# Larger weight chunks, one raw tile for a seven-product unit, and four such units in every column block of gate and up

## The chip, the cores and the metric

The kernel runs on one core of a Trainium2 chip. The metric is device time in microseconds (us) of one execution; the median of three runs of the kernel before is 2080.19 us.

## The reference

One layer of a decoder for 256 tokens (two tiles of 128, called t = 0, 1) with a model width D of 2048:

```python
f1 = swiglu(rms_norm(h, ffn1_pre_norm), ffn1_w_gate, ffn1_w_up, ffn1_w_down)   # D_FF = 5504
h = h + 0.5 * rms_norm(f1, ffn1_post_norm)
m = hybrid_token_mixer(rms_norm(h, mix_pre_norm), ...)    # u @ w_in, two linear attentions, w_branch_*, w_out
h = h + rms_norm(m, mix_post_norm)
f2 = swiglu(rms_norm(h, ffn2_pre_norm), ffn2_w_gate, ffn2_w_up, ffn2_w_down)
h = h + 0.5 * rms_norm(f2, ffn2_post_norm)
# swiglu(x, g, u, d) = (silu(x @ g) * (x @ u)) @ d
```

Everything is in float32. Nearly all of the arithmetic is in the products with the weight matrices: gate and up (2048 x 5504 each), down (5504 x 2048), w_in (2048 x 11280), the two branch matrices (1024 x 2048) and w_out (2048 x 2048).

## The kernel before, in words

**One product.** A product of a 128x128 piece of activations with a 128x512 block of weights in float32 is made of three matmuls (`mm3`, lines 157 to 159): x-high times w-high, x-low times w-high, x-high times w-low. So each weight block is needed as a high part and a low part. It is read by a DMA on the queue of SP into a tile `raw`; ACT copies it, rounded, into `whi` (line 151); DVE subtracts `whi` from `raw` into `wlo` (line 153). A chunk is two blocks, 512 KB (`RW = 2 * CB`); there are five buffers each of `raw`, `whi` and `wlo` (`RING = 5`). A buffer of `raw` is free again when DVE has made the low part, one of `whi`/`wlo` when the last matmul that reads it is done. SP issues its DMAs in order, each when its `raw` buffer is free.

**A column block.** The gate and up matrices are worked through in 11 blocks of 512 columns (the last of 384) by `gemm_pair`: four PSUM tiles c[t][i] (i = 0 gate, 1 up) gather 16 rows of 128x512 weight blocks, in eight units U0 to U7 of two rows each. A plain unit is four blocks (two rows of gate, two of up), 8 products, 24 matmuls.

**A unit of seven products.** For some units the 2x2 block product (two token tiles, two matrices) is made with 7 products in place of 8, in the manner of Strassen (`Blocks.seven`): 21 matmuls on PE, at the price of weight sums on DVE. Its four raw blocks lie in two tiles `ra` and `rb`, read by four DMAs of 256 KB. DVE adds two pairs (`wsum` 0 and 1, 128x1024), then replaces a raw block by a sum (128x512), then makes `wsum` 2 (128x512). ACT makes the high parts of `ra` (line 278), of wsum 0 and 1 (line 280), of `rb` (line 282) and of wsum 2 (line 284); DVE makes the low parts of `ra`, `rb` (128x1024 each) and of the three sums (128x1536), all in line 243, where every DVE add of the class `Blocks` is recorded. The sums of the activations (`hkhi`, `hklo`) are made once for a matrix. `SUMS = (2, 4, 6)` makes three units of a column block sevens, `FOUR = (2, 4, 5, 6)` four. Before, the column blocks 1 to 10 of each half-step take FOUR and SUMS in turn (in ffn1 the even ones FOUR, in ffn2 the odd ones); the first block has none. The units stand in the order U0, U1 (gate half), S2, U1 (up half), S4, U3 (gate half), S5, U3 (up half), S6, U7 with four sevens; S is a seven.

**After a column block**, `close` (DVE) adds the shared products, ACT applies silu, DVE multiplies gate and up into `hn`, PE transposes it (line 397, 8 transposes, in the next block) and ACT copies it to `hT` (line 709).

**The other stages.** `down_proj` does the same for the down matrix, in two halves of 1024 columns. The mixer computes w_in in pairs of column blocks (`two`, through `gemm_pair`); beside five of these pairs, marked `late`, PE, DVE, ACT and POOL also do the attention, as coroutines that `side.pump` advances. `out_proj` does w_out. The residual stream `h` (eight 128x512 tiles) stays in SBUF; in the mixer its room is lent out and it is read back from the DRAM tiles `away`.

**The order on each engine** is set when the program is built: a scheduler with a model of its own takes the instructions of all engines and writes each engine's list. At run time each engine goes through its list in order.

Of the kernel before, what the change touches and what calls it, by code (L numbers as in the profile page):

```python
# [27 lines left out]
RW = 2 * CB  # L28
STEPS = ((3, 2, 2, 2), (6, 1, 1, 1))
RING = 5  # L30
AHEAD = 3
# [55 lines left out]
def kernel(ctx: ExitStack, tc: tile.TileContext, a: dict, out: bass.AP):  # L87
# [22 lines left out]
    h = [[hpool.tile([P, CB], F32, name=f"h{t}_{n}") for n in range(4)] for t in range(NT)]  # L110

    away = [[dram.tile([P, CB], F32, name=f"away{t}_{n}") for n in range(4)] for t in range(NT)]
# [10 lines left out]

    def ring_alloc(w):
        hi, lo = [ring.tile([P, RW], F32R, tag=s, name=nm(s))[:, :2 * w]
                  .rearrange("p (i c) -> p i c", i=2) for s in ("whi", "wlo")]
        return [(hi, lo)]

    def wload(src: bass.AP, w: int, apart=False):
        raw = ring.tile([P, RW], F32, tag="raw", name=nm("raw"))[:, :2 * w].rearrange(  # L130
            "p (i c) -> p i c", i=2)
        for i in range(2) if apart else [slice(0, 2)]:
            nc.sync.dma_start(raw[:, i, :], src[:, i, :])
        return raw, apart

    def wchunk(src: bass.AP, w: int, alloc=ring_alloc, raw=None):


        raw, apart = raw or wload(src, w)
        parts = alloc(w)  # L140
        if len(parts) == 1:
            hi, lo = parts[0]
            for i in range(2) if apart else [slice(0, 2)]:
                split_into(hi[:, i, :], lo[:, i, :], raw[:, i, :])
            return [(hi[:, i, :], lo[:, i, :]) for i in range(2)]
        for i, (hi, lo) in enumerate(parts):
            split_into(hi, lo, raw[:, i, :])
        return parts
# [12 lines left out]
    def gemm_block(w_dram, c0, w, lhs, nkt=KT, held=None, raws=(), ready=()):  # L161
# [4 lines left out]
        raws, ready = list(raws), list(ready)  # L166
        nb = -(-w // CB)
        step = 2 // nb
        pss = [[ps_tile(f"mm{t}") for _ in range(nb)] for t in range(NT)]

        def chunk(k0, alloc):
            if ready:
                return ready.pop(0)
            raw = raws.pop(0) if raws else None
            src = w_dram[k0 * P:(k0 + step) * P, c0:c0 + w]
            return wchunk(src.rearrange("(k p) c -> p k c", p=P) if nb == 1 else
                          src.rearrange("p (n c) -> p n c", n=nb), w // nb, alloc, raw)

        def mm(t, k0, parts):
            for i, part in enumerate(parts):  # L180
                kt = k0 + i % step
                mm3(pss[t][i // step][:, :w // nb], lhs(t, kt), part, kt == 0, kt == nkt - 1)

        if held is None:
            for k0 in range(0, nkt, step):
                parts = chunk(k0, ring_alloc)
                for t in range(NT):
                    mm(t, k0, parts)
                side.pump()
        else:  # L190
            kept = []
            for i, k0 in enumerate(range(0, nkt, 2)):
                kept.append((k0, chunk(k0, ring_alloc if i < RING else held)))
                mm(0, *kept[-1])
                side.pump()
            for k in kept:
                mm(1, *k)
                side.pump()
            side.flush()
# [45 lines left out]
    class Blocks:  # L245
# [19 lines left out]
        def seven(self, u, end):  # L265
            w, k0 = self.w, 2 * u
            ra, rb = [ring.tile([P, RW], F32, tag="raw", name=nm("raw"))[:, :2 * w]
                      .rearrange("p (i c) -> p i c", i=2) for _ in range(2)]
            wsum, hi, lo = [row_tile(n, d)[:, :, :w] for n, d in
                            (("wsum", F32), ("wsumh", F32R), ("wsuml", F32R))]  # L270

            nc.sync.dma_start(ra[:, 0, :], self.block(0, k0))
            nc.sync.dma_start(ra[:, 1, :], self.block(1, k0 + 1))
            nc.sync.dma_start(rb[:, 0, :], self.block(1, k0))
            nc.sync.dma_start(rb[:, 1, :], self.block(0, k0 + 1))
# [4 lines left out]
            nc.scalar.activation(hi[:, 0:2, :], wsum[:, 0:2, :], AF.Copy)  # L280
            add(rb[:, 0, :], wsum[:, 0, :], ra[:, 1, :])
            nc.scalar.activation(bhi, rb, AF.Copy)  # L282
            summed = add(wsum[:, 2, :], rb[:, 0, :], rb[:, 1, :])
            last[0] = nc.scalar.activation(hi[:, 2, :], wsum[:, 2, :], AF.Copy)  # L284
# [4 lines left out]
            first, second, third = [[(part[0][:, i, :], part[1][:, i, :]) for i in range(n)]  # L289
                                    for part, n in (((ahi, alo), 2), ((bhi, blo), 2), ((hi, lo), 3))]  # L290
# [5 lines left out]
            self.product((0, 0), self.lhs(0, k0 + 1), second[1])  # L296
            side.pump()
            self.product("p6", self.part("s2", u), second[0], end)
            self.product("p5", self.part("d", u), third[0], end)
            self.product("p7", self.part("s3", u), third[1], end)  # L300
            self.product((1, 0), self.lhs(1, k0 + 1), third[2])
# [21 lines left out]
    def first_of(w_dram, c0, w=CB):  # L323
        def chunk(i):
            return wchunk(w_dram[2 * i * P:2 * (i + 1) * P, c0:c0 + w]
                          .rearrange("(k p) c -> p k c", p=P), w)
        return chunk

    def gemm_pair(ws, w, lhs, sums, ready=(), following=(), raws=(), sevens=SUMS,
# [11 lines left out]
        def split(i, k0):  # L341
            return wchunk(None, w, raw=raws.pop(0)) if raws else first_of(*ws[i], w)(k0 // 2)

# [11 lines left out]
        ready = list(ready)  # L355
        for j, (u, i) in enumerate(steps):
# [7 lines left out]
            parts = ready.pop(0) if ready else split(i, k0)  # L364
            if (u, i) == (nu - 1, 0) and sevens:
                ready = [split(1, k0)]
                b.share()
            for t in range(NT):
                b.plain((k0, k0 + 1), t, i, parts, u == nu - 1)
            side.pump()  # L370
        ready = [chunk(0) for chunk in following]
# [162 lines left out]
    def out_proj(w_dram, nkt, lhs, post, scale, pre, homes, following):  # L534
# [8 lines left out]
        def load(kt, hf, alloc=ring_alloc):  # L543
            return wchunk(w_dram[kt * P:(kt + 1) * P, hf * 1024:(hf + 1) * 1024]
                          .rearrange("p (n c) -> p n c", n=2), CB, alloc)

        def mm(t, n, kt, parts):
            if acc[t][n] is None:
                acc[t][n] = ps_tile(f"acc{t}{n}")
            mm3(acc[t][n], lhs(t, kt), parts[n % 2], kt == 0, kt == nkt - 1)  # L550

        order = [(kt, hf) for hf in range(2) for kt in range(2)]
        order += [(kt, hf) for kt in range(2, nkt - TAIL) for hf in range(2)]
        for i, (kt, hf) in enumerate(order):
            parts = load(kt, hf)
            if 6 <= i < 10:
# [5 lines left out]
                load_bcast(wpost[-1], post, i - 6, last[0])  # L562
            for t in range(NT):
                for n in (2 * hf, 2 * hf + 1):
                    mm(t, n, kt, parts)
            if i == 1:
                side.flush()
        tail = [[(kt, load(kt, hf, homes[hf * TAIL + i]))
                 for i, kt in enumerate(range(nkt - TAIL, nkt))] for hf in range(2)]

        for t in range(NT):
            ss = small.tile([P, 4], F32, tag="ss", name=nm("ss"))
            for n in range(4):
                for i, (kt, parts) in enumerate(tail[n // 2]):
# [12 lines left out]
    def down_proj(w_dram, nkt, lhs, sums_of, post, pre, wpost, ys, homes, following):  # L587
# [8 lines left out]
        def split(hf, kt, alloc=ring_alloc):  # L596
            return wchunk(w_dram[kt * P:(kt + 1) * P, hf * 1024:(hf + 1) * 1024]
                          .rearrange("p (n c) -> p n c", n=2), CB, alloc)
# [18 lines left out]
        ahead = []  # L617
        for hf in range(2):
# [6 lines left out]
            kt = 0  # L625
            while kt < n:
                u = kt // 2
                if kt % 2 == 0 and u + 1 in units and u + 1 not in parts:
                    parts[u + 1] = sums_of(u + 1)
                if u in units:  # L630
                    b.seven(u, u == units[-1])
                    kt += 2
                    continue
                chunk = ahead.pop(0) if ahead else split(hf, kt)
                if kt == 2 * units[-1] + 2:
                    ahead = [split(hf, kt + 1)]
                    b.share()
                if not hf and kt in (8, 9, 10, 11):
                    load_bcast(wpost[kt - 8], post, kt - 8, last[0])
                for t in range(NT):  # L640
                    for i in range(2):
                        b.plain((kt,), t, i, chunk[i:i + 1], kt == nkt - 1)
                if not hf and kt == 1:
                    side.flush()
                kt += 1
# [717 lines left out]
```

## Time and profile before

| | |
|---|---|
| runs | 2079.95, 2080.19, 2080.34 us |
| profiled execution | 2080.67 us, span 2078.8 us, granted clock of PE 0.999 |
| PE, matmuls | 2067.8 us busy, 99% |
| DVE | 1854.7 us busy, 89% |
| ACT | 1239.7 us busy, 60% |
| DMA | 412 MB, mean 198 GB/s |

The span is what the profile shows of the execution; the rest of its 2080.67 us, 1.9 us, lies around it. "Busy" of PE counts matmuls that overlap in the pipeline once. Rows of a timeline give the start, the duration, the engine, the line, and what was written from what; a duration of a pipelined instruction is longer than the step to the next start.

### The profile page before, as it was taken

To read this page: it belongs to the slowest core of one execution; us is meant where nothing else is said; L and a number is where in the kernel's file an instruction comes from. 1 tells how busy PE (TensorE), PEld (TensorE's weight loads), DVE (VectorE), ACT (ScalarE), POOL (GpSimd) and SP (SyncE) were. 2 spreads that over 40 slices of the span, in tenths; PEclk is the share of its full clock that TensorE was granted. 3 is DMA by queue.
4 is the path that set the end of the run, shared out by engine and by line. 5 is a ranking of instruction groups with operands and counts; after the bars stand their busy time and mean duration, and the time that the engine had idled before them with its cause. 6 is when DMAs were issued, how large, how long until landed. Compare 5 with 4: busy or idle time off the path is not lost.

```text
span 2078.8 us, 29319 instructions
## 1 busy us (share of the span) xinstructions
PE 2067.8 (99%) x10509; PEld 1721.1 (83%) x10509; DVE 1854.7 (89%) x2187; ACT 1239.7 (60%) x1670; POOL 40.6 (2%) x87
## 2 busy tenths in 40 slices
PE   9999999999999999999999999999999999999998
PEld 7888888898888888878888888888888888898886
DVE  7898999989999879989999897578999989999896
ACT  6555656565666576576655554465555655666663
POOL 1000000000000100000000000010000000000000
PEclk9999999999999999999999999999999999999999
DMA  8566656656667467555565666755666657576663
GB/s 267 183 210 199 211 188 194 214 183 226 208 195 233 153 192 232 163 168 188 174 203 186 184 221 214 220 179 172 222 200 186 209 186 224 165 239 201 198 208 132
DMA packets 200665, 412.23 MB, mean 198 GB/s; under 512 B 18036, under 2 KB 26423, under 8 KB 200520
## 3 DMA queue, kind: packets, MB, share of 16 engines
q1 hardware_dynamic: 194896, 401.80, 61.0%
q10 hardware_dynamic: 5624, 8.57, 1.3%
q8 instruction: 82, 1.34, 0.3%
q14 instruction: 63, 0.52, 0.1%
HBM read 406.11 MB, written 4.19 MB: 197 GB/s over the span
## 4 chain that ended last, share of the span: by engine, by line
PE 96%; ACT 1%; DVE 1%; issue 0%; DMA 0%; POOL 0%; SPq 0%; DVEq 0%; POOLq 0%; ACTq 0%
PE c L157 22%; PE c L159 21%; PE c L158 21%; PE p L159 5%; PE p L158 5%; PE p L157 5%; PE mm L157 3%; PE mm L159 3%; PE mm L158 3%; PE ps L397 2%; PE acc L157 1%; PE acc L158 1%; PE acc L159 1%; PE ps L905 0%; DVE h L510 0%
## 5 line engine op out<-in xcount | busy, mean ns | idle before, releaser
L151 ACT ACTIVATE whi<-raw 128x1024 fp32r<-128x1024 f32 (+3 forms) x498 | 510.6, 1033 | 279.8 <-PE c L158 114.7
L153 DVE TENSOR_TENSOR wlo<-raw,whi 128x1024 fp32r<-128x1024 f32 (+3 forms) x498 | 587.5, 1190 | 86.6 <-ACT whi L151 85.3
L157 PE MATMUL c<-whi,xhi 128*128 128x512 f32 (+1 forms) x1270 | 495.8, 391 | 0.5 <-DVE hq L849 0.3
L159 PE MATMUL c<-wlo,xhi 128*128 128x512 f32 (+1 forms) x1270 | 490.8, 387 | 0.0
L158 PE MATMUL c<-whi,xlo 128*128 128x512 f32 (+1 forms) x1270 | 490.5, 386 | 0.0
L243 DVE TENSOR_TENSOR wlo<-raw,whi 128x1024 fp32r<-128x1024 f32 (+1 forms) x252 | 294.5, 1203 | 11.9 <-ACT whi L278 6.3
L159 PEld LDWEIGHTS c<-wlo,xhi 128*128 128x128 f32 x1270 | 238.4, 188 | 47.2 <-DVE wlo L153 0.3
L157 PEld LDWEIGHTS c<-whi,xhi 128*128 128x128 f32 x1270 | 238.5, 188 | 46.9 <-issue 0.7
L158 PEld LDWEIGHTS c<-whi,xlo 128*128 128x128 f32 x1270 | 238.6, 188 | 44.9
L282 ACT ACTIVATE whi<-raw 128x1024 fp32r<-128x1024 f32 (+1 forms) x126 | 131.8, 1046 | 204.5 <-DVE raw L243 78.5
L243 DVE TENSOR_TENSOR wsuml<-wsum,wsumh 128x1536 fp32r<-128x1536 f32 (+1 forms) x126 | 218.0, 1730 | 33.7 <-ACT wsumh L284 33.6
L157 PE MATMUL c<-whi,hkhi 128*128 128x512 f32 x558 | 217.0, 389 | 0.0
L159 PE MATMUL c<-wlo,hkhi 128*128 128x512 f32 x558 | 216.8, 388 | 0.0
L158 PE MATMUL c<-whi,hklo 128*128 128x512 f32 x558 | 216.7, 388 | 0.0
L280 ACT ACTIVATE wsumh<-wsum 128x1024 fp32r<-128x1024 f32 (+1 forms) x126 | 131.5, 1044 | 108.6 <-DVE wsum L243 74.7
L278 ACT ACTIVATE whi<-raw 128x1024 fp32r<-128x1024 f32 (+1 forms) x126 | 131.4, 1043 | 100.2 <-PE c L158 84.7
L243 DVE TENSOR_TENSOR wsum<-raw,raw 128x1024 f32<-128x1024 f32 (+1 forms) x126 | 151.8, 1205 | 20.5 <-DMA raw<-in_ffn_w_down_dram 17.3
L159 PEld LDWEIGHTS c<-wlo,hkhi 128*128 128x128 f32 x558 | 104.8, 188 | 21.6
L158 PEld LDWEIGHTS c<-whi,hklo 128*128 128x128 f32 x558 | 104.8, 188 | 21.3
L157 PEld LDWEIGHTS c<-whi,hkhi 128*128 128x128 f32 x558 | 104.8, 188 | 21.3
L243 DVE TENSOR_TENSOR c<-c,psum 128x512 f32<-128x512 f32 (+1 forms) x135 | 86.6, 682 | 11.8 <-PE c L159 11.4
L243 DVE TENSOR_TENSOR wsum<-raw 128x512 f32<-128x512 f32 (+1 forms) x126 | 86.0, 683 | 3.6
(347 smaller groups left out, 3117.1 us busy)
## 6 DMA issues: line engine op xcount, KB each, us to landing
raw<-in_ffn_w_down_dram SPq DMA_DIRECT2D x124, 512.0 KB, 4.6
raw<-in_w_in_dram SPq DMA_DIRECT2D x104, 512.0 KB, 4.5
raw<-in_ffn_w_up_dram SPq DMA_DIRECT2D x97, 512.0 KB, 4.5
raw<-in_ffn_w_gate_dram SPq DMA_DIRECT2D x96, 512.0 KB, 4.7
raw<-in_ffn_w_gate_dram SPq DMA_DIRECT2D x128, 256.0 KB, 3.8
raw<-in_w_in_dram SPq DMA_DIRECT2D x128, 256.0 KB, 3.5
raw<-in_ffn_w_up_dram SPq DMA_DIRECT2D x126, 256.0 KB, 3.8
raw<-in_ffn_w_down_dram SPq DMA_DIRECT2D x96, 256.0 KB, 4.0
```

The lines of the kernel that those rows point to most:

```text
L151: last[0] = nc.scalar.activation(hi, src, AF.Copy)
L153: nc.vector.tensor_tensor(lo, src, hi.bitcast(F32), op=ALU.subtract)
L157: nc.tensor.matmul(ps, lhsT=xhi, rhs=whi, start=start, stop=False)
L158: nc.tensor.matmul(ps, lhsT=xlo, rhs=whi, start=False, stop=False)
L159: nc.tensor.matmul(ps, lhsT=xhi, rhs=wlo, start=False, stop=stop)
L243: return nc.vector.tensor_tensor(o, x, y, op=op)
L278: nc.scalar.activation(ahi, ra, AF.Copy)
L280: nc.scalar.activation(hi[:, 0:2, :], wsum[:, 0:2, :], AF.Copy)
L282: nc.scalar.activation(bhi, rb, AF.Copy)
L397: end = nc.tensor.transpose(dst_ps[:, i * P:(i + 1) * P], src[:, i * P:(i + 1) * P], ident)
```

## The change

Chunks grow from two blocks to four (`RW = 4 * CB`, 1 MB), and the buffers become fewer: three of `whi`/`wlo` (12 blocks where there were 10) and two of `raw` (8 blocks where there were 10). A plain unit is loaded into one raw tile by two DMAs of 512 KB, gate and up, and split by one ACT instruction and one DVE instruction of 128x2048. A seven has all four raw blocks in one tile: ACT copies three of them at once (line 291), then the fourth, which has become a sum (line 294), then the three weight sums at once (line 296); DVE makes the low parts of the four blocks at once. `h` is written to DRAM (`away2`, or taken from the input x again) after the first column block of each half-step, and its room serves as two more raw tiles, so there are four (16 blocks) from there until `residual()` in the second half of `down_proj`; in the mixer, in `out_proj` and in the first column block there are two. To make room, `hn` shares the tiles of `silu` and some other pools shrink. All ten column blocks of gate and up after the first take FOUR.

```diff
-RW = 2 * CB
+RW = 4 * CB
-RING = 5
-AHEAD = 3
+RING = 3
+RAWS = 2
+AHEAD = 2
...
+    def raw_tile(w):
+        turn[0] += 1
+        if roomy[0] and turn[0] % (RAWS + NT) >= RAWS:
+            raw = hpool.tile([P, RW], F32, tag="hold", name=nm("raw"), bufs=NT)
+        else:
+            raw = ring.tile([P, RW], F32, tag="raw", name=nm("raw"), bufs=RAWS)
+        return raw[:, :4 * w].rearrange("p (i c) -> p i c", i=4)
...
         def seven(self, u, end):
-            (ahi, alo), (bhi, blo) = ring_alloc(w) + ring_alloc(w)
-            nc.scalar.activation(ahi, ra, AF.Copy)
-            add(wsum[:, 0:2, :], ra, rb[:, 0:1, :].broadcast_to([P, 2, w]))
-            nc.scalar.activation(hi[:, 0:2, :], wsum[:, 0:2, :], AF.Copy)
-            add(rb[:, 0, :], wsum[:, 0, :], ra[:, 1, :])
-            nc.scalar.activation(bhi, rb, AF.Copy)
-            summed = add(wsum[:, 2, :], rb[:, 0, :], rb[:, 1, :])
-            last[0] = nc.scalar.activation(hi[:, 2, :], wsum[:, 2, :], AF.Copy)
+            raw = raw_tile(w)
+            for j, (i, k) in enumerate(((0, k0), (1, k0 + 1), (0, k0 + 1), (1, k0))):
+                load(raw, j, self.block(i, k))
+            hi, lo = ring_alloc(w)[0]
+            nc.scalar.activation(hi[:, 0:3, :], raw[:, 0:3, :], AF.Copy)
+            add(wsum[:, 0:2, :], raw[:, 0:2, :], raw[:, 3:4, :].broadcast_to([P, 2, w]))
+            add(raw[:, 3, :], wsum[:, 0, :], raw[:, 1, :])
+            nc.scalar.activation(hi[:, 3, :], raw[:, 3, :], AF.Copy)
+            summed = add(wsum[:, 2, :], raw[:, 3, :], raw[:, 2, :])
+            last[0] = nc.scalar.activation(shi, wsum, AF.Copy)
             with tc.issue_after(summed.ins):
-                add(alo, ra, ahi.bitcast(F32), ALU.subtract)
-            add(blo, rb, bhi.bitcast(F32), ALU.subtract)
-            add(lo, wsum, hi.bitcast(F32), ALU.subtract)
+                add(lo, raw, hi.bitcast(F32), ALU.subtract)
+            add(slo, wsum, shi.bitcast(F32), ALU.subtract)
...
-                        (FOUR if f0 // CB % 2 == fours else SUMS) if f0 else ())
+                        FOUR if f0 else ())
                 else:
                     g = gemm_block(a[pre + "_w_gate"], f0, w, xl, held=held, ready=ready)
+                    for t in range(NT):
+                        nc.sync.dma_start(away2[t], hrow[t])
...
+                roomy[0] = True
...
+            def residual():
+                roomy[0] = False
+                new_h()
+                for t in range(NT):
+                    nc.sync.dma_start(hrow[t], a["x"][t * P:(t + 1) * P, :].rearrange(
+                        "p (n c) -> p n c", c=CB) if begin else away2[t])
```

The order on ACT in column block 6 of ffn1 (four sevens before and after), from the high part of S2's first blocks to S4's last. Before, `raw_498`/`raw_499` are S2's two raw tiles and `raw_514`/`raw_515` those of S4; `hT` is the copy of the transposed block 5:

```order
L278 ACTIVATE whi_503_2447<-raw_498_2438 128x1024
L728 ACTIVATE silu_484_2371<-c00_415_2029,r_65_414 128x512
L728 ACTIVATE silu_485_2373<-c10_417_2031,r_67_421 128x512
L280 ACTIVATE wsumh_501_2441<-wsum_500_2440 128x1024
L282 ACTIVATE whi_505_2449<-raw_499_2439 128x1024
L284 ACTIVATE wsumh_501_2441<-wsum_500_2440 128x512
L151 ACTIVATE whi_512_2488<-raw_511_2486 128x1024
L278 ACTIVATE whi_519_2513<-raw_514_2504 128x1024
L709 ACTIVATE hT_486_2375<-ps_493_2408 128x4x128
L709 ACTIVATE hT_486_2375<-ps_494_2414 128x4x128
L282 ACTIVATE whi_521_2515<-raw_515_2505 128x1024
```

After, `raw_350` is S2's raw tile, `raw_360` that of S4, `raw_366` that of U3:

```order
L291 ACTIVATE whi_354_2208<-raw_350_2200 128x1536
L771 ACTIVATE silu_339_2136<-c10_292_1826,r_57_396 128x512
L291 ACTIVATE whi_364_2263<-raw_360_2255 128x1536
L746 ACTIVATE hT_340_2138<-ps_345_2169 128x4x128
L746 ACTIVATE hT_340_2138<-ps_346_2175 128x4x128
L294 ACTIVATE whi_354_2208<-raw_350_2200 128x512
L296 ACTIVATE wsumh_352_2202<-wsum_351_2201 128x1536
L164 ACTIVATE whi_367_2297<-raw_366_2294 128x2048
L294 ACTIVATE whi_364_2263<-raw_360_2255 128x512
```

S2's remaining high parts stood ahead of everything of S4; now S4's first copy and the two of hT stand ahead of them.

PE at the same S2, its first four products. Before:

```order
L157 MATMUL p1_507_2461<-whi_503_2447,xhi0_1_107 128x512
L158 MATMUL p1_507_2461<-whi_503_2447,xlo0_2_108 128x512
L159 MATMUL p1_507_2461<-wlo_504_2448,xhi0_1_107 128x512
L157 MATMUL c01_490_2381<-whi_503_2447,hkhi_85_524 128x512
L158 MATMUL c01_490_2381<-whi_503_2447,hklo_86_525 128x512
L159 MATMUL c01_490_2381<-wlo_504_2448,hkhi_85_524 128x512
L157 MATMUL c00_489_2380<-whi_505_2449,xhi0_1_107 128x512
L158 MATMUL c00_489_2380<-whi_505_2449,xlo0_2_108 128x512
L159 MATMUL c00_489_2380<-wlo_506_2450,xhi0_1_107 128x512
```

and after:

```order
L170 MATMUL p1_356_2218<-whi_354_2208,xhi0_3_97 128x512
L171 MATMUL p1_356_2218<-whi_354_2208,xlo0_4_98 128x512
L170 MATMUL c01_342_2142<-whi_354_2208,hkhi_66_483 128x512
L171 MATMUL c01_342_2142<-whi_354_2208,hklo_67_484 128x512
L170 MATMUL c00_341_2141<-whi_354_2208,xhi0_3_97 128x512
L171 MATMUL c00_341_2141<-whi_354_2208,xlo0_4_98 128x512
L170 MATMUL p6_357_2219<-whi_354_2208,hkhi_66_483 128x512
L172 MATMUL p1_356_2218<-wlo_355_2209,xhi0_3_97 128x512
L172 MATMUL c01_342_2142<-wlo_355_2209,hkhi_66_483 128x512
L172 MATMUL c00_341_2141<-wlo_355_2209,xhi0_3_97 128x512
```

Seven matmuls with high parts now stand ahead of the first one that needs S2's low part; before there were two.

DVE in a late pair of the mixer, the one beside the first attention output (`on`). Before, `raw_1745` and `raw_1746` are its first seven's raw tiles, `raw_1761` and `raw_1762` the second's:

```order
L243 TENSOR_TENSOR wlo_1753_8420<-raw_1746_8409,whi_1752_8419 128x1024
L987 SCALAR_TENSOR_TENSOR on_1741_8387<-ps_1736_8374,r_1740_8385,h1_0_85 128x256 x2
L243 TENSOR_TENSOR wsuml_1749_8412<-wsum_1747_8410,wsumh_1748_8411 128x1536
L153 TENSOR_TENSOR wlo_1760_8459<-raw_1758_8456,whi_1759_8458 128x1024
L243 TENSOR_TENSOR wsum_1763_8476<-raw_1761_8474,raw_1762_8475 128x1024
L243 TENSOR_TENSOR raw_1762_8475<-wsum_1763_8476,raw_1761_8474 128x512
```

After, `raw_1238` is the first seven's tile and `raw_1251` the second's:

```order
L259 TENSOR_TENSOR wlo_1243_7547<-raw_1238_7538,whi_1242_7546 128x2048
L1041 SCALAR_TENSOR_TENSOR on_1231_7507<-ps_1224_7491,r_1230_7505,h0_810_4883 128x256 x2
L259 TENSOR_TENSOR wsuml_1241_7541<-wsum_1239_7539,wsumh_1240_7540 128x1536
L1041 SCALAR_TENSOR_TENSOR on_1237_7523<-ps_1232_7510,r_1236_7521,h1_811_4884 128x256 x2
L166 TENSOR_TENSOR wlo_1250_7585<-raw_1248_7581,whi_1249_7584 128x2048
L259 TENSOR_TENSOR wsum_1252_7601<-raw_1251_7600 128x1024
```

The instructions stand in nearly the same order, but with two raw tiles `raw_1251` is the room of `raw_1238`: its DMAs can go out only after the first row, and the last row waits for them.

More of the change, by code (lines that the diff above doesn't have):

```diff
@@ L266, in seven @@
             w, k0 = self.w, 2 * u
[L267 to L274, printed above, removed]
@@ L295, in seven @@
             self.product((0, 1), self.part("s4", u), first[1])
-            self.product((0, 0), self.lhs(0, k0 + 1), second[1])
+            self.product((0, 0), self.lhs(0, k0 + 1), first[2])
             side.pump()
[L298 to L301, printed above, removed]
+            self.product("p6", self.part("s2", u), first[3], end)
+            self.product("p5", self.part("d", u), second[0], end)
+            self.product("p7", self.part("s3", u), second[1], end)
+            self.product((1, 0), self.lhs(1, k0 + 1), second[2])
             side.pump()
@@ L363, in gemm_pair @@
             k0 = 2 * u
[L364 to L367, printed above, removed]
+            if i == 0:
+                cuts = ()
+                if raws:
+                    raw, cuts = raws.pop(0)
+                    hi, lo = ring_alloc(w)[0]
+                    parts = [(hi[:, j, :], lo[:, j, :]) for j in range(4)]
+                else:
+                    parts = ready or split(load_unit(ws, u, w), w)
+                    ready = None
+                if u == nu - 1 and sevens:
+                    b.share()
+            for c in cuts[i] if cuts else ():
+                split_into(hi[:, c, :], lo[:, c, :], raw[:, c, :])
             for t in range(NT):
-                b.plain((k0, k0 + 1), t, i, parts, u == nu - 1)
+                b.plain((k0, k0 + 1), t, i, parts[2 * i:2 * i + 2], u == nu - 1)
             side.pump()
-        ready = [chunk(0) for chunk in following]
+        ready = following and following()
         for i in range(2 if sevens else 0):
@@ L549, in mm, with all_of @@
                 acc[t][n] = ps_tile(f"acc{t}{n}")
[L550 to L556, printed above, removed]
+            mm3(acc[t][n], lhs(t, kt), parts[n], kt == 0, kt == nkt - 1)
+        def all_of(ns, *chunks):
+            for kt, parts in chunks:
+                for t in range(NT):
+                    for n in ns:
+                        mm(t, n, kt, parts)
+        begun = []
+        for kt in range(2):
+            begun.append((kt, chunk(kt)))
+            all_of((0, 1), begun[-1])
+        side.flush()
+        all_of((2, 3), *begun)
+        for kt in range(2, nkt - TAIL):
+            parts = chunk(kt)
+            if 3 <= kt < 7:
                 if not free:
@@ L561, in out_proj @@
                 wpost.append(free.pop(0))
[L562 to L569, printed above, removed]
+                load_bcast(wpost[-1], post, kt - 3, last[0])
+            all_of(range(4), (kt, parts))
+        tail = [(kt, chunk(kt, homes[i])) for i, kt in enumerate(range(nkt - TAIL, nkt))]
         for t in range(NT):
@@ L624, in down_proj @@
             units = sorted(DSUMS + DMORE[hf])
[L625 to L628, printed above, removed]
+            for kt in range(0, n, 2):
+                u, m = kt // 2, min(2, n - kt)
+                if u + 1 in units and u + 1 not in parts:
                     parts[u + 1] = sums_of(u + 1)
```

261 lines of the change are left out of this document (144 added, 117 removed).

## The prediction

> **What bounds the kernel now.** I read the page's busy times first, then the chain that ended last, then what PE waits for.
>
> ```profile
> span 2078.8 us, 29319 instructions
> PE 2067.8 (99%) x10509; PEld 1721.1 (83%) x10509; DVE 1854.7 (89%) x2187; ACT 1239.7 (60%) x1670; POOL 40.6 (2%) x87
> PEclk9999999999999999999999999999999999999999
> PE 96%; ACT 1%; DVE 1%; issue 0%; DMA 0%; POOL 0%; SPq 0%; DVEq 0%; POOLq 0%; ACTq 0%
> ```
>
> PE holds 96% of the chain at full granted clock. The longest single waits of PE in the whole run are small:
>
> ```profile
> PE ps L1303 <- POOL idle L1298: 1.3, 1, 1.3
> PE ps L965 <- ACT state L975: 0.4, 1, 0.4
> PE c L157 <- DVE hq L849: 0.3, 1, 0.3
> ```
>
> So the time can fall only through fewer matmuls, and rises with every new wait of PE: 2067.8 of 2078.8 us is PE, and of the other 11 us the change touches little (the settling and the output at the end keep their instructions).
>
> DVE is the second limit. Two neighbouring column blocks of ffn1, three sevens (first) and four (second); the columns are PE, PEld, DVE, ACT, POOL, clock, DMA share, GB/s:
>
> ```profile
> 145.37:187.75 42.38, 42.38 (x193) 35.18 (x192) 38.63 (x39) 25.60 (x31) 0.00 (x0) 1.00 0.60 188
> 187.75:229.47 41.72, 41.72 (x189) 34.62 (x189) 39.99 (x41) 23.09 (x28) 0.00 (x0) 1.00 0.65 213
> ```
>
> The windows end where the transposes of `hn` end; the block lengths are thus 42.38 and 41.72 us. PE is busy throughout both. DVE works 38.63 us in the one and 39.99 in the other, where it has 1.73 us left.
>
> **The gain: matmuls removed.** Ten more sevens replace ten plain units, each with one product, three matmuls, less: 27 of 128x512 and 3 of 128x384 (ffn2's last block). What a matmul costs on a saturated PE is the step from start to start, not its duration of 0.39:
>
> ```profile
> 192.39 0.39 PE L157 MATMUL p<-whi,hkhi 128*128 128x512 f32 x1
> ...
> 194.89 0.39 PE L159 MATMUL c<-wsuml,xhi 128*128 128x512 f32 x1
> ```
>
> Eleven steps in 2.50 us, 0.227 each. The difference of the two blocks above, 0.66 us, is three matmuls by 0.22: four sevens gave their whole gain there. 27 x 0.227 + 3 x 0.17 (three quarters) = 6.6 us. Nothing else lies on PE's path to be removed, so 2080.2 - 6.6 = 2073.6 is the floor.
>
> **DVE and ACT in a block of four sevens.** The rows by form for the second window:
>
> ```profile
> L153 DVE TENSOR_TENSOR wlo<-raw,whi 128x1024 fp32r<-128x1024 f32 x9 | 10.9, 1216 | 0.0
> L243 DVE TENSOR_TENSOR wsuml<-wsum,wsumh 128x1536 fp32r<-128x1536 f32 x4 | 7.0, 1755 | 1.4 <-ACT wsumh L284 1.4
> L243 DVE TENSOR_TENSOR raw<-wsum,raw 128x512 f32<-128x512 f32 x4 | 2.8, 692 | 0.1
> L282 ACT ACTIVATE whi<-raw 128x1024 fp32r<-128x1024 f32 x4 | 4.2, 1057 | 11.0 <-DVE raw L243 3.9 <-issue 3.9 <-PE c L159 3.1
> L284 ACT ACTIVATE wsumh<-wsum 128x512 fp32r<-128x512 f32 x3 | 1.8, 615 | 0.0
> ```
>
> On DVE 692, 1216 and 1755 ns for 512, 1024 and 1536 columns: 0.53 per 512 more, so 128x2048 is estimated at 2.29 us. Instructions that follow each other overlap: a group of two of 1024 lasts 2.35 and the next starts 2.27 after its start, 1.13 each.
>
> ```profile
> 192.38 2.35 DVE L243 TENSOR_TENSOR wlo<-raw,whi 128x1024 fp32r<-128x1024 f32 x2
> 194.65 1.22 DVE L153 TENSOR_TENSOR wlo<-raw,whi 128x1024 fp32r<-128x1024 f32 x1
> ```
>
> Merging two of 1024 into one of 2048 so saves about 0.07 us, eight times a block: 0.55 us, and DVE comes to 39.4 of 41.7. Off PE's path this is worth nothing by itself; it pays for the waits below. [...]
>
> What changes more is where DVE waits. Before, 1.4 us a block for the copy of the third sum. Now ACT's lists in the order above put S4's first copy ahead of S2's last one, and S4's copy needs a `whi` buffer; with three, that is U0's. Count from the end of U0 on PE (zero). ACT starts about 0.10 after the last reader of the high part ends, as here:
>
> ```profile
> 194.66 0.39 PE L158 MATMUL c<-wsumh,xlo 128*128 128x512 f32 x1
> ...
> 195.15 1.06 ACT L280 ACTIVATE wsumh<-wsum 128x1024 fp32r<-128x1024 f32 x1 [0.28 <-PE c L158]
> ```
>
> That reader starts two steps before the end, so ACT starts at 0.04. The copy of 1536 columns takes about 1.39 (1.06 for 1024 and 0.43 for 512 more, less the overlap with the next), the two `hT` copies 0.95, S2's last copy of 512 columns 0.62, and DVE's 128x2048 2.29 more: S2's low part is there at 5.3 to 5.4. PE has meanwhile 8 transposes and 12 matmuls of U1, then the seven high matmuls of S2 that the new order puts ahead:
>
> ```profile
> 186.88 0.87 PE ps L397 x8
> ```
>
> 0.87 + 19 x 0.227 = 5.2. PE waits about 0.16 us. (In the old order, with two ahead, it would be 0.87 + 14 x 0.227 = 4.05 and a wait of 1.3.) The same count gives the low parts of S4, S5 and S6 0.4 to 0.6 us to spare. Eighteen blocks follow another block of four: 18 x 0.16 = 2.9 us. Both sides are sums of some five terms, so I bound it by 0 and 0.4 a block, 0 to 8 us.
>
> **Two raw tiles in the mixer, `out_proj` and the first blocks.** Loads wait for DVE to free a raw tile, now as before, but a mixer pair has 8 blocks of room for 10 and frees 4 at a time. The reload of one tile, by the times to landing:
>
> ```profile
> raw<-in_w_in_dram SPq DMA_DIRECT2D x104, 512.0 KB, 4.5
> raw<-in_w_in_dram SPq DMA_DIRECT2D x128, 256.0 KB, 3.5
> ```
>
> Two of 512 KB, or four of 256 KB that SP issues about 0.38 apart, land in some 4.6 to 5.4 us. Then a plain unit needs ACT's copy (1.9) and DVE's 2.29: 8.8 to 9.6. A seven needs two adds, the copy of the fourth block and the low part, 1.25 + 0.73 + 0.62 + 2.29: 9.5 to 10.3. Two tiles serve two units of PE, 48 or 45 or 42 matmuls, 10.9 or 10.2 or 9.5 us. It just fits where ACT and DVE are free at once; where DVE is full it does not. It is full in the attention stage:
>
> ```profile
> 835.00:1000.00 165.00, 164.59 (x1345) 133.07 (x1333) 156.53 (x234) 110.14 (x190) 7.09 (x12) 1.00 0.55 170
> ```
>
> 95% of 165 us. In the late pair shown in the order above, the second seven's load starts when the first's low part is made; until it lands, 4.6 to 5.4 us later, DVE has the two `on` (1.6), the sums' low part (1.67) and one plain low part (2.2), 5.5 us when all stand ready, 3.9 when the attention's are done: a hole of 0 to 1.3 us. Before it ran without one from there on:
>
> ```profile
> 906.04 1.22 DVE L153 TENSOR_TENSOR wlo<-raw,whi 128x1024 fp32r<-128x1024 f32 x1
> 907.17 1.22 DVE L243 TENSOR_TENSOR wsum<-raw,raw 128x1024 f32<-128x1024 f32 x1
> ```
>
> Ten pairs by 0 to 0.8 us, since only what outlasts PE's lead counts: 0 to 8, and I take 1 because attention matmuls stretch PE's side of these pairs. `out_proj` has 24 matmuls to each chunk (5.4 us, two tiles 10.9 against 9.6), the start of the kernel was waiting for DMA anyway, the last part of `down_proj` likewise has plain chunks: together 0 (0 to 2). The copies of `h` to DRAM and back, 2 MB each, go out beside a DMA share of 0.65: nothing, unless SP's queue holds the loads behind them.
>
> **Sum.** -6.6 + 2.9 + 1 + 0 = -2.7. Against the profiled 2080.67 that is 2078.0; the median is 0.5 lower, so 2077.5 us.
>
> **The rivals.**
> - A, all hidden: the reordered matmuls cover S2's low part and the raw tiles reload in time. For it: PE waits for nothing today. 2073.6 to 2075.
> - B, the mixer starves for raw tiles: what speaks for it is the reload plus the split at 9.5 to 10.3 against 9.5 to 10.9, and a DVE at 95%; against it, that PE in the late pairs does attention too. Ten pairs by 1 us and 2 for the other stages: +12 - 6.6 + 1 = 2086.6.
> - C, DVE becomes the bound of gate and up (the other side): it has 39.4 us of work in 41.7, and all blocks are alike now, without one of three sevens (DVE 38.63 of 42.38) between in which to catch up. From 2.3 us of waiting in a block on, DVE sets its length. S2's last copy, at 3.0 us from zero, is a wait of DVE, and three more sevens each have one. At 3.3 us: 1 us by 20 blocks, less 6.6: 2093.6. Against it: before it waited 1.4.
> - D, the new sevens just do not pay: DVE's waits come to some 0.35 us on PE in each of the 20 blocks: 2080.
>
> [...]
>
> **How the numbers follow.** Chances: forecast (2075 to 2080) 0.42, A 0.22, B 0.20, C 0.11, D 0.05. A measurement of this kernel tells 0.2%, 4.2 us, from nothing: faster is below 2076.0, slower above 2084.4. Faster: A and 0.18 of the forecast, 0.40. Slower: 0.17 of B and 0.09 of C, 0.26. Within: 0.34. The range runs from the floor less a little, 2073, to 2090, which leaves out most of C and the far part of B; the forecast's own is 2073.6 to 2082.
>
> **What would show it.** Right: PE's first low matmul of S2 (line 172, `p<-wlo`) waits 0.1 to 0.3 us for DVE in most blocks, blocks of 41.7 to 42.0 us, DVE at 94% there, line 166 or 259 waiting now and then for a raw DMA in the mixer. Wrong: blocks over 42.4 us with PE waiting for DVE in several sevens (C), PE idle between 690 and 1300 us, in the mixer (B), or blocks of 41.7 without any wait (A).

## The result, and the profile after

The changed kernel takes 2138.09 us (median of 4 runs, 2138.04 to 2139.94) against 2080.27 for the kernel before on the same chip: a ratio of 1.0279, 95% interval 1.0261 to 1.0296. It is 58 us slower, where 2077.5 was forecast and 2090 was the upper end.

The page's busy times and the chain by engine, after:

```profile
span 2136.3 us, 27567 instructions
PE 2093.8 (98%) x10479; PEld 1709.7 (80%) x10479; DVE 1877.4 (88%) x1852; ACT 1219.5 (57%) x1315; POOL 49.9 (2%) x87
PE 74%; DVE 10%; DMA 8%; ACT 4%; issue 2%; SPq 1%; POOL 0%; DVEq 0%; ACTq 0%; POOLq 0%
```

PE holds 74% of the chain where it held 96%. DVE, DMA and ACT have taken the rest, and that trio is the path of a raw tile: load, copy, low part. What PE waits for (in total, times, longest), and what ACT waits for:

```profile
PE p L172 <- DVE wlo L259: 5.3, 8, 1.6
...
PE mm L170 <- ACT xhi L164: 3.4, 1, 3.4
PE c L172 <- DVE wlo L166: 3.2, 4, 1.6
```

```profile
ACT whi L164 <- DMA raw<-in_w_in_dram: 85.0, 38, 10.6
...
ACT whi L291 <- DMA raw<-in_w_in_dram: 52.7, 19, 6.8
```

Before, the longest row of the second kind was this one:

```profile
ACT whi L151 <- DMA raw<-in_w_in_dram: 11.5, 14, 2.1
```

PE's listed waits come to some 32 us (2 before) and do not add up to the loss; matmuls that start a little late, or run at the lower clock told at the end, count as "busy" PE (2093.8 us, 26.0 more than before with 30 matmuls fewer) and are the rest. So I read the loss by stage, from the start of the first matmul of each stage in the timeline (lengths in us; "mixer q" is the first column blocks of the mixer, "pairs" the column pairs beside the attention, "gates" the rest of the mixer up to w_out, "ffn2" from its second column block to its last matmul; the names of the other kernels are explained with the experiments):

| kernel | ffn1 | mixer q | pairs | gates | w_out, first block of ffn2 | ffn2 |
|---|---|---|---|---|---|---|
| before | 693.7 | 49.7 | 328.6 | 225.5 | 135.5 | 637.0 |
| after | 708.4 | 53.9 | 349.3 | 234.4 | 135.4 | 645.0 |
| alt_new | 708.3 | 52.6 | 348.4 | 233.8 | 135.8 | 647.3 |
| fours_old | 691.2 | 49.7 | 327.9 | 225.5 | 135.6 | 633.9 |
| mixer_room | 709.1 | 54.3 | 332.2 | 226.0 | 135.6 | 645.8 |
| two_raws | 740.6 | 52.9 | 346.1 | 232.8 | 135.7 | 683.8 |
| late_residual | 699.3 | 49.7 | 345.9 | 234.5 | 135.6 | 639.8 |
| halves | 692.4 | 48.7 | 329.4 | 225.5 | 135.3 | 634.2 |
| split_only | 693.7 | 48.9 | 337.9 | 232.8 | 135.3 | 635.8 |

Of the 58 us, 29.6 lie in pairs and gates, 4.2 in mixer q, 14.7 in ffn1, 8.0 in ffn2 and 1.0 after the last matmul. The chain in order of time shows the round of a raw tile bare where down_proj of ffn1 ends and the mixer begins:

```profile
689.92 6.55 DMA raw<-in_w_in_dram
...
696.56 1.93 ACT whi L164
...
698.51 2.30 DVE wlo L166
700.83 4.99 DMA raw<-in_w_in_dram
...
705.90 1.79 ACT whi L164
```

One load, one copy, one low part, the next load: each waits for the one before, 11 us a round. The other tile makes the same round half a turn later, and PE still had work of the tail in it (10.77 of these 10.91 us); it ran out behind the last copy, where it waited 3.41 us for an `xhi` that stood behind that copy in ACT's list.

A gate and up block is 42.30 us now (41.72 with four sevens before). The rows by form of DVE and the window:

```profile
188.67:230.97 42.30, 42.30 (x190) 34.25 (x189) 40.96 (x34) 24.56 (x22) 0.00 (x0) 1.00 0.62 200
```

```profile
L259 DVE TENSOR_TENSOR wlo<-raw,whi 128x2048 fp32r<-128x2048 f32 x4 | 9.2, 2293 | 0.9 <-ACT whi L294 0.9
L166 DVE TENSOR_TENSOR wlo<-raw,whi 128x2048 fp32r<-128x2048 f32 x4 | 9.1, 2283 | 0.0
```

DVE works 40.96 and waits 0.9 for S2's last copy; steps of 0.03 to 0.04 us between dependent adds are most of the rest.

### The profile page after: what moved, and what is told of

Its sections match the earlier page's. It is cut to its first block, busy times and chain, and to the rows that moved or that the text cites. A ratio compares the mean times of both kernels' runs of the same rounds, so it can differ in the third digit from the quotient of the medians.

```text
span 2136.3 us, 27567 instructions
## 1 busy us (share of the span) xinstructions
PE 2093.8 (98%) x10479; PEld 1709.7 (80%) x10479; DVE 1877.4 (88%) x1852; ACT 1219.5 (57%) x1315; POOL 49.9 (2%) x87
## 4 chain that ended last, share of the span: by engine, by line
PE 74%; DVE 10%; DMA 8%; ACT 4%; issue 2%; SPq 1%; POOL 0%; DVEq 0%; ACTq 0%; POOLq 0%
PE c L172 16%; PE c L170 16%; PE c L171 16%; DMA raw<-in_w_in_dram 5%; PE p L172 5%; PE p L171 4%; PE p L170 4%; DVE wlo L259 2%; DVE wlo L166 2%; DMA raw<-in_ffn_w_down_dram 2%; PE mm L170 2%; PE mm L172 2%; PE mm L171 2%; ACT whi L164 2%; PE ps L421 2%
## 5 line engine op out<-in xcount | busy, mean ns | idle before, releaser
L164 ACT ACTIVATE whi<-raw 128x2048 fp32r<-128x2048 f32 (+4 forms) x244 | 450.8, 1848 | 326.6 <-DMA raw<-in_w_in_dram 85.0
L166 DVE TENSOR_TENSOR wlo<-raw,whi 128x2048 fp32r<-128x2048 f32 (+4 forms) x244 | 536.2, 2200 | 107.9 <-ACT whi L164 105.4
L259 DVE TENSOR_TENSOR wlo<-raw,whi 128x2048 fp32r<-128x2048 f32 (+1 forms) x136 | 307.3, 2260 | 33.5 <-ACT whi L294 33.2
L291 ACT ACTIVATE whi<-raw 128x1536 fp32r<-128x1536 f32 (+1 forms) x136 | 200.1, 1471 | 213.5 <-issue 63.2
L259 DVE TENSOR_TENSOR wsum<-raw 128x1024 f32<-128x1024 f32 (+3 forms) x272 | 256.9, 945 | 26.3 <-DMA raw<-in_w_in_dram 14.6
L170 PE MATMUL c<-whi,hkhi 128*128 128x512 f32 (+1 forms) x568 | 222.0, 391 | 6.1 <-ACT hkhi L164 3.6
L171 PE MATMUL c<-whi,hklo 128*128 128x512 f32 (+1 forms) x568 | 221.8, 391 | 0.6 <-DVE hklo L166 0.6
L172 PE MATMUL c<-wlo,hkhi 128*128 128x512 f32 (+1 forms) x568 | 221.5, 390 | 0.0
L296 ACT ACTIVATE wsumh<-wsum 128x1536 fp32r<-128x1536 f32 (+1 forms) x136 | 199.9, 1470 | 32.9 <-DVE wsum L259 32.0
L259 DVE TENSOR_TENSOR raw<-wsum,raw 128x512 f32<-128x512 f32 (+1 forms) x136 | 92.9, 683 | 3.7
```

The source lines that it names most:

```text
L164: last[0] = nc.scalar.activation(hi, src, AF.Copy)
L166: nc.vector.tensor_tensor(lo, src, hi.bitcast(F32), op=ALU.subtract)
L170: nc.tensor.matmul(ps, lhsT=xhi, rhs=whi, start=start, stop=False)
L171: nc.tensor.matmul(ps, lhsT=xlo, rhs=whi, start=False, stop=False)
L172: nc.tensor.matmul(ps, lhsT=xhi, rhs=wlo, start=False, stop=stop)
L259: return nc.vector.tensor_tensor(o, x, y, op=op)
```

## The experiments

Theory R: raw tiles come back too late, because two tiles of four blocks are loaded, copied, split and freed in turn. Beside it theory G, that not the amount of room but the grain of four blocks is what costs. Rivals of both: the additional sevens overload DVE (F), or S2's late copy in ACT's order is what costs in gate and up (J).

**The sevens alone.** The kernel before, with one edit:

```diff
-                        (FOUR if f0 // CB % 2 == fours else SUMS) if f0 else ())
+                        FOUR if f0 else ())
```

> The kernel before (two-block chunks, five buffers) with four sevens in every column block of gate and up; nothing else of the change. If the sevens themselves overload DVE (40.0 us of work and 1.4 of waits in 41.7): gate and up blocks of 42.4 us or more, 2080 or above. If the cost of the change lies in its chunks and raw tiles (theories R and G): the full gain of 6.6 us, 2073 to 2075, blocks of 41.7 throughout.

Measured: 2075.97 us, ratio 0.9978 (0.9968 to 0.9987), 4.1 us less between the medians and a little above the 2073 to 2075 expected. Its profiled execution, one of its shortest, has a span of 2072.4, 6.4 us less than before. Its gate and up blocks:

```profile
186.56:228.28 41.72, 41.72 (x190) 34.61 (x189) 41.22 (x42) 24.17 (x29) 0.00 (x0) 1.00 0.63 202
```

41.72 although DVE is at 41.22: in the trace the 30 matmuls are worth what was counted, and F falls for the old chunks.

**The chunks without the sevens.** The changed kernel with four and three sevens in turn.

```diff
-                        FOUR if f0 else ())
+                        (FOUR if f0 // CB % 2 == (0 if begin else 1) else SUMS) if f0 else ())
```

> The changed kernel with four and three sevens in turn, as before. If the sevens are what costs (DVE full in blocks that are all alike): most of the 58 us comes back, below 2095. If the chunks and raw tiles cost: gate and up hardly move, 2136 to 2142.

Measured: 2134.94, ratio 1.026 (1.0243 to 1.0277), 1 us below what was expected if the chunks cost, and 3 less than the changed kernel, which the intervals do not separate. So 55 of the 58 us come with the chunks, and with them the ten additional sevens do not gain their 6 us. But gate and up alone are cured. Two neighbouring blocks, of three and of four sevens:

```profile
146.73:189.11 42.38, 42.38 (x193) 35.19 (x192) 38.74 (x31) 23.98 (x22) 0.00 (x0) 1.00 0.66 220
189.11:230.83 41.72, 41.72 (x190) 34.61 (x189) 38.90 (x33) 23.11 (x20) 0.00 (x0) 1.00 0.55 180
```

These are the lengths of before. From the first to the last transposes of `hn`, gate and up of ffn1 take 411.3 us here and before, 414.9 in the changed kernel. So in gate and up neither the sevens (fours_old) nor the chunks (this run) cost anything alone; the loss there needs both, and there F holds with the new chunks. The two down_proj stages lose more than in the changed kernel (13.3 and 10.3 us, where it loses 10.1 and 4.4); why, no run shows.

**Less raw room, old chunks.** In the kernel before, `bufs=4` at both places that allocate `raw`.

> The kernel before with four raw tiles of two blocks in place of five: 8 blocks of raw room, as the changed kernel has in the mixer, but freed two at a time. Theory R (raw room is what is short): the mixer and the end of down_proj wait for loads, 2090 to 2120. Theory G (the room would do; what costs is that a tile of four blocks is loaded, copied, split and freed as one): 2080 to 2085.

Measured: 2089.97 (2085.82 to 2091.45), ratio 1.0043 (1.0028 to 1.0058): 10 us, at the foot of what theory R gives and above what G gives. Eight blocks of room are fewer than ten, but in pieces of two they cost 10 us, not 58.

**More raw room in the mixer.** The changed kernel, with the room of `xlo` lent to raw tiles during the ten pairs; the low part of the activations is left out of the mixer there.

```diff
+        if lent and turn[0] % 4 >= RAWS:
+            raw = tpool.tile([P, RW], F32, tag=lent[turn[0] % 4 - RAWS], name=nm("raw"))
...
     def mixer(x, rs, ready, following):
+        x = x[0], x[0], x[2]
```

> The changed kernel with four raw tiles in place of two in the ten pairs of the mixer: the room of xlo is lent to the raw tiles, and the matmuls there take xhi where they took xlo (so the low part of the activations is left out of the mixer's results; matmuls, copies and sums are the same in number and shape). Theory R: the ten pairs lose most of their 29 us of delay, 2105 to 2115. If the delay comes from DVE's order and the long split instructions instead: 2130 to 2140.

Measured: 2114.15, ratio 1.0159 (1.0144 to 1.0174). Pairs and gates fall from 583.7 to 558.2 us, against 554.1 before, so 25.5 of their 29.6 us come back; the other stages stay within 1 us of the changed kernel. Room for chunks of this size is what the mixer was short of.

**Room for longer in down_proj.** `if hf and u == 16: residual()` in place of `u == 6`.

> The changed kernel with four raw tiles kept longer in down_proj: h comes back at unit 16 of the second half, not at unit 6. Theory R: most of the 15 us that the two down_proj stages lose comes back, 2123 to 2131, and the clock of 0.95 to 0.98 between 600 and 800 us rises. If those 15 us come from the held tiles of the tail instead: 2136 to 2140.

Measured: 2115.58, ratio 1.0173 (1.0156 to 1.019): 22.5 us back, more than the 15 expected. ffn1 gives 9, mixer q 4, the pairs 3, ffn2 5. The first load of w_in goes out at 675.2 us in place of 689.9, so the tail and the start of the mixer are less late; how the gain of the later stages comes about was not taken apart.

**Two raw tiles everywhere** (`roomy` never set).

> The changed kernel with two raw tiles everywhere (h's room is not used for raw tiles). Theory R: gate, up and the first part of down_proj now starve like the mixer, by 2 to 4 us in each of the 20 column blocks: 2180 to 2230. If the room is enough where the attention does not load DVE: 2138 to 2150.

Measured: 2203.18 in its one run, 65 us above the changed kernel. ffn1 is 32 us longer and ffn2 39; of each, 16 us lie in the ten blocks of gate and up, 1.6 a block, and the rest in down_proj. Two tiles of four blocks are too few without the attention too.

**The same eight blocks, in halves.** The raw room of two tiles becomes four tiles of two blocks; the loads, copies and low parts of a unit are made for each half apart. The buffers of the high and low parts stay as in the changed kernel.

```diff
-            raw = ring.tile([P, RW], F32, tag="raw", name=nm("raw"), bufs=RAWS)
+            halves = [ring.tile([P, RW // 2], F32, tag="raw", name=nm("raw"), bufs=2 * RAWS)
+                      for _ in range(2)]
...
-            nc.scalar.activation(hi[:, 0:3, :], raw[:, 0:3, :], AF.Copy)
+            nc.scalar.activation(hi[:, 0:2, :], raw[:, 0:2, :], AF.Copy)
+            nc.scalar.activation(hi[:, 2, :], raw[:, 2, :], AF.Copy)
...
-                add(lo, raw, hi.bitcast(F32), ALU.subtract)
+                add(lo[:, 0:2, :], raw[:, 0:2, :], hi[:, 0:2, :].bitcast(F32), ALU.subtract)
+            add(lo[:, 2:4, :], raw[:, 2:4, :], hi[:, 2:4, :].bitcast(F32), ALU.subtract)
```

> The changed kernel with the raw room where there are two tiles cut into four tiles of two blocks: the same 8 blocks, but a plain unit's gate half and up half, and the two halves of a seven, are loaded, copied, split and freed apart (two ACT and two DVE instructions in place of one each). The buffers of the high and low parts stay at three of four blocks. If it is the number of blocks of raw room that is short: 2125 to 2140. If it is that the room is freed in pieces of four blocks, so that DMA, ACT and DVE take turns: at least half of the 44 us lost in the mixer and at the end of down_proj come back, 2095 to 2115.

Measured: 2079.1, ratio 0.9991 (0.9982 to 1.0): 59 us back, far more than expected. Against fours_old, which has the same matmuls, 3 us may stay, which the intervals do not quite separate. In its profiled execution (2075.95, the shortest of ten) every stage is within 1 us of before or below it, with the same number of raw blocks. The rest of the change is still in it (the copies of `h`, the shared tiles, three buffers of `whi`/`wlo`), so none of that costs more than these few us. A gate and up block of it, for which two of the four raw tiles are still whole:

```profile
185.50:227.20 41.70, 41.70 (x190) 34.59 (x189) 40.83 (x41) 24.90 (x29) 0.00 (x0) 1.00 0.62 201
```

DVE has as much work as in the changed kernel (40.83 and 40.96 us), in 41 instructions for 34, and the 0.58 us are gone.

**Only the instructions in halves.** As halves, but both halves lie in one raw tile, so that its room comes free as a whole.

```diff
-            halves = [ring.tile([P, RW // 2], F32, tag="raw", name=nm("raw"), bufs=2 * RAWS)
-                      for _ in range(2)]
+            raw = ring.tile([P, RW], F32, tag="raw", name=nm("raw"), bufs=RAWS)
+            halves = [raw[:, :RW // 2], raw[:, RW // 2:]]
```

> The halves kernel (loads, ACT copies and DVE low parts in pieces of two blocks) but with both halves in one raw tile, so that the room of four blocks comes free as a whole, as in the changed kernel. If the release of the whole tile is what costs in the mixer and at the end of down_proj: only gate and up get better (about 8 to 12 us), 2122 to 2132. If the length of the ACT and DVE instructions is what costs: 2079 to 2090, like halves.

Measured: 2095.9, ratio 1.0074 (1.0059 to 1.0089). If the release were what costs I had 2122 to 2132, if the length of the instructions 2079 to 2090; the truth lies between, nearer the second. 42 of the 59 us come with shorter instructions (and the loads that they take apart), 17 with the release of the room in halves. By stage: ffn1, mixer q and ffn2 need only the shorter instructions (693.7, 48.9 and 635.8); pairs and gates, where DVE is shared with the attention, need both (570.7, between 583.7 and 554.9).

**Halves, and h later.** Halves with `u == 16`.

> The halves kernel with h coming back at unit 16 of the second half of down_proj. Halves has 2.0 us of steps that are too long between 600 and 700 us, and late_residual gave 22.5 us to the changed kernel; with room freed in halves most of that is no longer there to be had: 2074 to 2079, and no more than 3 us below halves.

Measured: 2074.98, ratio 0.9976 (0.9966 to 0.9986), span 2073.1; 4 us below halves, where I had at most 3. This and fours_old are below the kernel before by the same 0.2% (5.7 and 4.1 us between medians), about what the removed matmuls were counted at.

**S2's copy first.** The changed kernel with an order on ACT: the first copy of a seven after the last raw copy of the seven before.

```diff
+            with tc.issue_after(self.prev.ins) if self.prev else nullcontext():
+                nc.scalar.activation(hi[:, 0:3, :], raw[:, 0:3, :], AF.Copy)
...
+            self.prev = nc.scalar.activation(hi[:, 3, :], raw[:, 3, :], AF.Copy)
```

> The changed kernel with the first copy of each seven put behind the last raw copy of the seven before (on ACT, S2's 512-column copy now stands ahead of S4's 1536-column one). If the wait at S2's low part is the joint that the prediction counted (0.18 and 0.11 us at the first two low matmuls of each block): blocks of 41.9 to 42.1 in place of 42.3, 4 to 8 us less, 2130 to 2134. If DVE as a whole sets the length of a block: no change, 2136 to 2140.

Measured: 2139.82, ratio 1.0288 (1.0273 to 1.0303): no gain, as expected if DVE as a whole sets the length. One early block is shorter (41.71), the later ones are longer (42.45 from 273.85 us on). There DVE waits 0.5 us for the last raw copy, where it was 0.9, and 0.9 us for the copies of the sums, where it was none. Making that one copy earlier moved the wait, so J falls as a cure.

**A sum on POOL.** In the changed kernel `wsum[:, 2, :]` is made by `nc.gpsimd.tensor_tensor`, and the low part of the raw blocks is no longer held behind it in DVE's order.

> The changed kernel with the third weight sum of every seven (128x512, 0.69 us on DVE, four in a block) made on POOL, which is idle in gate and up. If DVE sets the length of a gate and up block (41.0 busy and 0.9 of waits in 42.3): blocks of 41.7 and 8 to 12 us less, 2126 to 2132. If the late copy on ACT sets it: 2136 to 2142. If POOL is slow or shares DVE's access: slower than 2140.

Measured: 2189.07, ratio 1.052 (1.0502 to 1.0538). Gate and up blocks take 44.0 us. This does not test DVE's load, since the price is elsewhere: 1.35 us on POOL for 0.69 on DVE, and DVE slowed down (below).

## Why the prediction was wrong

**The gain (-6.6)** was right in the trace, where fours_old has a span 6.4 us shorter; its medians give 4.1, and 6.6 lies at the edge of their interval.

**DVE in a block of four sevens (39.4 of 41.7)** was mis-sized, by how the row was read. DVE runs ahead of PE (the low part of S2's sums, begun at 186.98 us, is first read by a matmul at 193.53), so the window 187.75 to 229.47 does not hold the DVE work of just its own block. The two windows together do: 38.63 + 39.99 = 78.62 for one block of three and one of four sevens. A seven costs DVE three adds and the sums' low part more than a plain unit, 1.25 + 0.73 + 0.61 + 1.67 = 4.26 in steps; so four sevens are (78.62 + 4.26) / 2 = 41.4, and not 40. Measured: 41.22 in fours_old, 40.96 after. (The same sum over the two windows of alt_new, 77.64, gives 40.95.) Merging took off 0.3, not 0.55.

**S2's low part (0.16 us a block)** was right as a place and nearly as a size, and wrong as the price of a block. These are the steps there:

```profile
234.90 0.39 PE L170 MATMUL p<-whi,hkhi 128*128 128x512 f32 x1
235.31 0.50 PE L172 MATMUL p<-wlo,xhi 128*128 128x512 f32 x1
```

0.41 us from start to start in place of 0.23: 0.18 late. But the whole block loses 0.58, at several places. With DVE at 41 of 41.7 us, its 0.9 of waits is already more than there is. Rival C had this mechanism, that DVE sets the block once no block of three sevens stands between in which to catch up: alt_new gives DVE such blocks again and the loss is gone, while copy_first shortens the one wait and it is not. C's threshold (2.3 us of waits) was wrong since DVE's work was counted 1.6 us too low, and its price (1 us) too high. From the first to the last transposes of `hn`, gate and up take 414.9 us after and 411.3 before in ffn1, 414.4 and 410.8 in ffn2: with the 3.3 us gained in each, 13.8 us are lost (the narrow last blocks lose more than 0.58), where 2.9 were counted.

**Two raw tiles (+1, bounds 0 to 8)** was the step that failed. The measured price is 29.6 us in pairs and gates alone, and with mixer q (4.2) and the two down_proj stages (10.1 and 4.4) 48 us. Only w_out cost nothing, as counted (135.4 and 135.5 with the first block of ffn2). The parts were about right: from the chain of the mixer,

```profile
1223.73 2.30 DVE wlo L166
...
1226.06 0.33 SPq L150
...
1226.43 0.43 SPq L150
...
1226.90 4.73 DMA raw<-in_w_in_dram
```

5.6 us from the release to the landing, where I had 4.6 to 5.4. What was wrong was to set a sum of services, 8.8 to 10.3 us, against PE's 9.5 to 10.9 for two units and to call the difference slack. That sum is what a round takes at the least: in the pairs the shortest from release to release is 9.2 us for a plain unit and 10.4 for a seven. But of the 56 rounds that can be followed there 17 took over 13 us, up to 22. ACT and DVE also serve the other tile and the attention, each in the order of its list, and I added no queueing. PE's use of the high and low parts is not what held these rounds up: in the pairs ACT's copies of raw blocks waited 82.7 us for loads of w_in and 2.6 us for PE. In one round of the pairs DVE began the low part 4.3 us after ACT's copy had ended, with attention in between, and the round took 14.2:

```profile
915.12 1.91 ACT L164 ACTIVATE whi<-raw 128x2048 fp32r<-128x2048 f32 x1
```

```profile
914.77 1.14 DVE L1145 SCALAR_TENSOR_TENSOR lcl<-ident,lc,lch 128x128 fp32r<-128x128 f32 x4
...
920.76 0.69 DVE L944 TENSOR_TENSOR hqT<-hqT,hfT 128x512 f32<-128x512 f32 x1
921.36 2.28 DVE L166 TENSOR_TENSOR wlo<-raw,whi 128x2048 fp32r<-128x2048 f32 x1
```

The kernel before had five tiles of two blocks, so by estimate a round of about 13 us (PE's 9.5 to 10.9 for eight blocks, taken for ten) for 7 us of service (4.5 to land, 1.06 on ACT, 1.22 on DVE). Rival B named this (2086.6) but was priced with 1 us a pair; it was 3. "The last part of down_proj: 0 to 2" failed in the same way. At 645 us, for one, ACT had waited 3.94 us for a load at the head of its list, with the small copies of activations (`hkhi`) behind it, and PE waited 1.72 us for one of those.

**Was the room or the grain the cause?** It is the two together, and either cures it: with more room of the same grain most of the mixer's loss is gone (mixer_room), and with the same room of a finer grain nearly all loss is gone (halves). The short supply arises because each round is serial; halving the instructions lets ACT begin when half has landed and DVE when half is copied, which by my estimate takes up to half of 1.92 and half of 2.30, 2.1 us, off a plain unit's round, and separate tiles let the next load start earlier. That the overlap inside a tile is how split_only gains its 42 us is argued, not shown. The shortest rounds of a plain unit agree in part: 7.4 to 8.1 us there, 9.2 to 9.4 in the changed kernel; those of a seven are as long in both (10.5 and 10.4). ACT's waits for loads of w_in in the pairs fall from 82.7 us in the changed kernel to 46.5 in split_only and 36.0 in halves.

## What to carry to other kernels

A buffer is worth what its round allows: release to landing, plus each engine's turn with what is queued before it, against the time that the consumer takes for all buffers (in the pairs 9.2 to 22 us against 9.5 to 10.9). Merging instructions and transfers lengthened each turn (ACT's copy from 1.06 to 1.92 us, DVE's low part from 1.22 to 2.29) and freed room later, so two large buffers starved a consumer that four halves of the same bytes fed with next to no wait (2138.09 and 2079.1 us). To read a helper engine's load from a window, take windows over a full period of the work, since an engine that runs ahead does its work for a block in the window of another (39.99 us of DVE read from one window, 41.4 from two).

## What was not expected of the hardware

PE's clock fell after some of the waits. After the wait of 1.60 us at 764.6 the steps of one 128x512 matmul go from 0.23 to 0.43 us:

```profile
764.63 0.50 PE L172 MATMUL c<-wlo,xhi 128*128 128x512 f32 x1 [1.60 <-DVE wlo L166]
764.97 0.39 PE L170 MATMUL c<-whi,xhi 128*128 128x512 f32 x1
...
766.26 0.63 PE L171 MATMUL c<-whi,xlo 128*128 128x512 f32 x1
766.69 0.63 PE L172 MATMUL c<-wlo,xhi 128*128 128x512 f32 x1
```

The granted clock from 765.3 to 768.5 us is 0.52. Before the last matmul there are four such stretches in the changed kernel, three of 3.4 us (from 649.4, 765.4 and 867.8 us) and one of 6.8 (from 707.4, where PE was still waiting), and none in the kernel before. By an estimate from their lengths, half of some 16 us of work, they cost 8 us at most. The last waits ahead of the three were 1.6 to 2.1 us long, that around the fourth 3.4; waits of 1.5 us that ended at 685 and 720, of 1.6 at 793 and of 1.8 at 2073 were followed by none.

DVE slowed down beside POOL. In pool_sum the 128x2048 subtraction takes 2.28 us where POOL is idle and longer where POOL's 128x512 sum runs beside it. The mean of a seven's is 2.71, where a seven's in a gate and up block of the changed kernel took 2.29; one that began at 298.24 us, while POOL was busy up to 299.31, took 3.22, and one that began 0.56 after POOL's sum took 2.87:

```profile
305.81 2.87 DVE L259 TENSOR_TENSOR wlo<-raw,whi 128x2048 fp32r<-128x2048 f32 x1 [0.70 <-ACT whi L294]
...
310.28 2.28 DVE L166 TENSOR_TENSOR wlo<-raw,whi 128x2048 fp32r<-128x2048 f32 x1
```

```profile
305.25 1.29 POOL L295 TENSOR_TENSOR wsum<-raw 128x512 f32<-128x512 f32 x1 [5.94 <-issue]
```
